# A hybrid pooling and Mamba-2 step on one core: the state-space chunk stage in one written order on all five engines, and the tail's gating moved into PSUM

## The chip, the cores and the metric

The kernel runs on one core of a Trainium2 chip. The metric is device time in microseconds (us) of one execution; a time is the median of several runs. Engines are named as in the profile: PE (TensorE), DVE (VectorE), ACT (ScalarE), POOL (GpSimd) and SP (SyncE, which here only issues loads).

## What is computed

One layer of a decoder for 1024 prompt rows and 64 sample rows, in float32. Cut to what the change concerns:

```
u_pool, z_pool, z_ssm, xbc, dt, g = split(h @ w_in)
P = (pool_mix(u_pool) * silu(z_pool)) @ w_pool_out
# state-space part: chunks of 128 rows, per group of 8 heads
att   = (C B^T) * exp(-(decay differences, lower triangle)) * dt
y     = att @ x  +  (C * exp(cumulated decay)) @ state
state = state * exp(last) + B^T @ (weight * dt * x)
v = (y + d_skip * x) * silu(z_ssm)
S = rmsnorm(v, ssm_norm_g) @ w_ssm_out
m = sigmoid(g_pool) * P + sigmoid(g_ssm) * S
out = x + gate * (m @ w_o);   then a final rmsnorm
```

## The kernel before

Data lies transposed: channels on the 128 partitions, 1088 rows (1024 + 64) along the free axis. Float32 products are made from three matmuls, high part by high, high by low and low by high (L360 to L362), so every operand is first split into a high and a low part: a copy on ACT, then a subtraction on POOL or DVE.

The program goes through adaLN and gates, the large projections, convolution and pooling, the **chunk stage** (about 826 to 1138 us of the profile), the **tail** (to 1201) and the output product.

*Chunk stage.* There are 4 groups of 8 heads and 8 chunks each, 32 chunks. One chunk's work, `chunk(g, c)`, is a generator of four steps: load xb (x, B and C) and the decay tile `dec`; exponentials (`cE` L1398, POOL's mask in `far` L1193, eight `exps` L1202 on ACT); turn (PE transposes x and B and makes B by C, L118 and L1409), weigh (`xd` L1418, `ps` L1419, `xw` L1421), mix (`dec` L1422 and `cE` L1424 are multiplied in place), low parts (`xwl` L1425, `btl` L1426), skip (`xD` L1429, ACT); then `inner` (PE, L1214 and L1217), the state update (PE L1435 to L1437, POOL L1442, DVE L1444), the sum (`v` L1448) and `finish` (DVE L1368, ACT L1369 and L1378, POOL L1370 to L1379), which leaves y split into Y. After a group's last chunk its state is transposed back and stored from an `xD` buffer (L1456, L1457).

Between these, PE makes **products**: blocks of 384, 352 and 352 columns, 12 matmuls each. The first 24 blocks are P (`P_unit`, evicted by DVE with a multiply, L1624), the following 72 belong to S of groups 0 to 2 (`S_unit`; group 0 copied by ACT, L1642; later ones added by DVE, L1645). A block rotates through three PSUM buffers, a chunk's own tiles through five others. `xd`, `xw`, `xwl`, `bt` and `btl` have one buffer each, `cE`, `xD` and the state two, `xb`, `dec` and `sz` three.

Only PE follows the written order here (`in_line`). Where DVE, ACT, POOL and SP put their instructions is decided by a scheduler, by what it expects to be ready, and by `behind`, which places a few of them after an engine's earlier work. Products are drawn by 2.56 blocks a chunk, four ahead of the first.

*Tail.* For each of eight 128-row slabs m, S of group 3 is multiplied (three blocks) and added to the sum `acc[m]` (a `G` tile; L1789), multiplied by gains that come from rstd in PSUM and the gate rows `R` (L1780, L1795), and P's part is added by POOL (L1796). The result is split for the output product (`m_split`, L1759 to L1771, its 64 sample columns in `sh`), and the output weights are loaded and split (`wo_split`, L1752 and L1753). The rstd of all rows is spread over the partitions by matmuls with nine diagonal tiles, which DVE makes (L1732). PE and DVE follow the written order in this stage.

Of the kernel before, what the change touches and what calls it, by code (L numbers as in the profile page):

```python
# [20 lines left out]
P = 128  # L21
# [25 lines left out]
def tile_pool_ssd_step(  # L47
# [1318 lines left out]
    def finish(g, o, S, v, sz):  # L1366

        V.tensor_tensor(v, v, sz, ALU.mult)  # L1368
        act(sz, v, AF.Square)  # L1369
        nc.gpsimd.tensor_tensor(sz[:, 0:2], sz[:, 0:2], sz[:, 2:4], ALU.add)  # L1370
# [6 lines left out]
        yhc = yh[g][:, :, o:o + S]  # L1377
        act(yhc, v, AF.Copy)  # L1378
        nc.gpsimd.tensor_tensor(yl[g][:, :, o:o + S], v, yhc.bitcast(F32), ALU.subtract)  # L1379

    def sample_end(g):
        sz = ckt([P, 4, P], "sz", 3)[:, :, :NS]
        load(sz, z_d[g][:, :, SEQ:])
        v = ckt([P, 4, P], "v")[:, :, :NS]
        load(v, ys_d[g])
        finish(g, SEQ, NS, v, sz)

    def chunk(g, c):
        o = c * P
        xb = ckt([P, 6, P], "xb", 3)  # L1390
        load(xb, xbc_d[g][:, :, o:o + P])
        Bf, Cf = xb[:, 4], xb[:, 5]
        dec = ckt([P, 8, P], "dec", 3)
        decays(dec, g, c)
        yield
        if c > 0:
            cE = ckt([P, 8, P], "cE")
            act(cE, dec, AF.Exp, scale=-1.0)  # L1398
        far(dec, c)
        exps(dec, g, c)  # L1400
        yield
        sz = ckt([P, 4, P], "sz", 3)
        load(sz, z_d[g][:, :, o:o + P])
        px = PB()
        for q in range(4):
            turn_r(px[:, q * P:(q + 1) * P], xb[:, q])
        pbc = PB()
        turn_r(pbc[:, :P], Bf)
        mm(pbc[:, P:2 * P], Bf, Cf, start=True, stop=True)  # L1409

        bth, btl = (ck.tile([P, P], F32R, tag=t, name=nm(t), bufs=1) for t in ("bt", "btl"))
        act(bth, pbc[:, :P], AF.Copy)
        if c > 0:
            act(pbc[:, 2 * P:3 * P], Cf, AF.Copy)
        pxv = px.rearrange("p (h d) -> p h d", d=64)
        heads = slice(8 * g, 8 * g + 8)
        xd = ckt([P, 8, 64], "xd", 1)
# [5 lines left out]
        if c > 0:  # L1423
            V.tensor_tensor(cE, cE, pbc[:, 2 * P:3 * P].unsqueeze(1).to_broadcast([P, 8, P]), ALU.mult)  # L1424
# [3 lines left out]
        for q in range(4):  # L1428
            act(xD[:, q], xb[:, q], AF.Copy, scale=Dv[:, 4 * g + q:4 * g + q + 1])  # L1429
# [512 lines left out]
```

## Time and profile before

| | |
|---|---|
| median of 3 runs | 1300.18 us (1298.1 to 1300.95) |
| the profiled execution | 1301.8 us |
| its span, first to last instruction | 1300.1 us |
| granted TensorE clock, mean | 0.994 |
| PE busy | 1258.6 us (97%) |
| DVE, ACT, POOL busy | 913.3, 709.5, 682.1 us |
| HBM traffic | 179 GB/s over the span |

Busy times are averages over stages with different limits, and matmuls overlap, so 97% does not say where PE stood still. Rows of a stretch of the span show that better: how much of 20 us PE was busy, at which clock, and how busy DVE, ACT and POOL were in the same 20 us. Where PE was held up, the chain of waits (from the last instruction back to what released each step) names the operation that came last.

### The profile page before, as it was taken

The page shows a single profiled execution, that of the slowest core. Times are in us where ns is not written, and L with a number is a line of the kernel's source. Part 1 is how long each engine was busy: PE and PEld are TensorE (multiplying, and loading weights), DVE is VectorE, ACT ScalarE, POOL GpSimd, SP SyncE. Part 2 cuts the span into 40 slices and gives each one's busy share as a digit, 9 for nine tenths or more (in the row PEclk, how much of TensorE's full clock was granted, in tenths as well). Part 3 has the DMA queues.
Part 4 walks back from the last instruction along what each step waited for, and adds up shares of the span by engine and source line. Part 5 has one row for each costly group of instructions (what it writes and reads, how often), then busy time and mean ns, then how long its engine had stood idle before and what let it go on. Part 6 is the DMA issues. An engine that isn't in the chain of part 4 may idle for free.

```text
span 1300.1 us, 26439 instructions
## 1 busy us (share of the span) xinstructions
PE 1258.6 (97%) x9771; PEld 1177.4 (91%) x9771; DVE 913.3 (70%) x1581; ACT 709.5 (55%) x1676; POOL 682.1 (52%) x555
## 2 busy tenths in 40 slices
PE   7999999999999999999999999999899999989998
PEld 6779999989999999998989899989899999989786
DVE  4685778866978678775757655587677889478533
ACT  4665356375656564546455454777797878122211
POOL 1007668677869776664344444255475657266000
PEclk9999999999999999999999999999999999999999
DMA  9736345465455544444645565998666665284421
GB/s 333 241 116 224 119 153 171 142 206 166 151 183 198 157 159 128 158 138 125 192 142 173 155 178 161 341 320 285 215 202 199 191 210 163 74 300 165 156 89 49
DMA packets 225731, 234.92 MB, mean 181 GB/s; under 512 B 30369, under 2 KB 177009, under 8 KB 225594
## 3 DMA queue, kind: packets, MB, share of 16 engines
q1 hardware_dynamic: 155808, 159.01, 38.8%
q10 hardware_dynamic: 69794, 74.22, 16.7%
q8 instruction: 77, 1.26, 0.4%
q14 instruction: 52, 0.43, 0.1%
HBM read 158.67 MB, written 74.62 MB: 179 GB/s over the span
## 4 chain that ended last, share of the span: by engine, by line
PE 75%; DVE 6%; DMA 6%; issue 5%; ACT 4%; POOL 3%; ACTq 0%; SPq 0%; POOLq 0%; DVEq 0%
PE ps L609 6%; PE ps L610 6%; PE ps L611 6%; PE mm L609 6%; PE mm L611 6%; PE mm L610 6%; PE mm L361 5%; PE mm L360 5%; PE mm L362 5%; PE ps L1214 2%; PE ps L1888 2%; PE ps L1890 2%; PE ps L1889 2%; POOL wlo L169 2%; PE ps L1217 2%
## 5 line engine op out<-in xcount | busy, mean ns | idle before, releaser
L169 POOL TENSOR_TENSOR wlo<-rawA,whi 128x512 fp32r<-128x512 f32 x120 | 185.6, 1552 | 185.1 <-ACT whi L166 101.2
L169 POOL TENSOR_TENSOR wlo<-raw,whi 128x512 fp32r<-128x512 f32 x92 | 151.0, 1649 | 126.9 <-ACT whi L166 97.3
L360 PE MATMUL mm<-Y,whi 128*128 128x352 f32 (+1 forms) x480 | 161.2, 336 | 2.9 <-DVE G L1789 2.7
L361 PE MATMUL mm<-Y,whi 128*128 128x352 f32 (+1 forms) x480 | 158.5, 330 | 2.7 <-POOL Y L1379 1.6
L362 PE MATMUL mm<-Y,wlo 128*128 128x352 f32 (+1 forms) x480 | 158.1, 329 | 0.0
L611 PE MATMUL mm<-Y,wlo 128*128 128x272 f32 x496 | 143.5, 290 | 3.7 <-POOL wlo L169 3.3
L609 PE MATMUL ps<-Y,whi 128*128 128x272 f32 x496 | 144.5, 291 | 2.1 <-ACT o L809 1.5
L609 PE MATMUL mm<-Y,whi 128*128 128x272 f32 x496 | 146.3, 295 | 0.2 <-ACT whi L166 0.2
L610 PE MATMUL ps<-Y,whi 128*128 128x272 f32 x496 | 143.1, 289 | 0.0
L610 PE MATMUL mm<-Y,whi 128*128 128x272 f32 x496 | 142.8, 288 | 0.0
L611 PE MATMUL ps<-Y,wlo 128*128 128x272 f32 x496 | 142.6, 288 | 0.0
L166 ACT ACTIVATE whi<-rawA 128x512 fp32r<-128x512 f32 x125 | 78.2, 626 | 97.4 <-PE ps L610 43.0
L1057 DVE SCALAR_TENSOR_TENSOR GA<-GA,cvT,GA 128x1112 f32<-128x1112 f32 x72 | 125.5, 1747 | 0.3
L166 ACT ACTIVATE whi<-raw 128x512 fp32r<-128x512 f32 x96 | 58.7, 626 | 92.7 <-DVE raw L555 42.8
L611 PEld LDWEIGHTS mm<-Y,wlo 128*128 128x128 f32 x496 | 93.4, 188 | 5.6 <-POOL wlo L169 4.6
L609 PEld LDWEIGHTS ps<-Y,whi 128*128 128x128 f32 x496 | 93.3, 188 | 3.8 <-ACT o L809 1.7
L360 PEld LDWEIGHTS mm<-Y,whi 128*128 128x128 f32 x480 | 91.3, 190 | 5.3 <-DVE G L1789 3.1
L361 PEld LDWEIGHTS mm<-Y,whi 128*128 128x128 f32 x480 | 91.3, 190 | 5.1 <-POOL Y L1379 1.9
L609 PEld LDWEIGHTS mm<-Y,whi 128*128 128x128 f32 x496 | 93.3, 188 | 2.1 <-issue 0.8
L610 PEld LDWEIGHTS mm<-Y,whi 128*128 128x128 f32 x496 | 93.4, 188 | 0.7 <-issue 0.6
L611 PEld LDWEIGHTS ps<-Y,wlo 128*128 128x128 f32 x496 | 93.5, 188 | 0.2 <-issue 0.2
L610 PEld LDWEIGHTS ps<-Y,whi 128*128 128x128 f32 x496 | 93.3, 188 | 0.3 <-issue 0.2
(454 smaller groups left out, 3852.4 us busy)
## 6 DMA issues: line engine op xcount, KB each, us to landing
rawA<-in_w_in SPq DMA_DIRECT2D x46, 512.0 KB
dec<-acs_d SPq DMA_DIRECT2D x32, 512.0 KB
xbc<-GA ACTq DMA_DIRECT2D x24, 512.0 KB
xb<-xbc SPq DMA_DIRECT2D x32, 384.0 KB
rawA<-in_w_in SPq DMA_DIRECT2D x32, 256.0 KB
pw<-in_w_ssm_out ACTq DMA_DIRECT2D x32, 256.0 KB
ws<-ph ACTq DMA_DIRECT2D x32, 256.0 KB
ws<-pw SPq DMA_DIRECT2D x32, 256.0 KB
```

The costliest lines, as they stand in the source:

```text
L166: ins = act(hi[:, :, :ncols], raw[:, :, :ncols], AF.Copy)
L169: (eng or nc.gpsimd).tensor_tensor(lo[:, :, :ncols], raw[:, :, :ncols], hi[:, :, :ncols].bitcast(F32), ALU.subtract)
L360: mm(ps[:, :n], a, rh[k][:, o:o + n], start=(k == 0), stop=False)
L361: mm(ps[:, :n], a, rl[k][:, o:o + n], start=False, stop=False)
L362: mm(ps[:, :n], b, rh[k][:, o:o + n], start=False, stop=(k == nk - 1))
L609: mm(p, hi, ah, start=(k == 0), stop=False)
L610: mm(p, hi, al, start=False, stop=False)
L611: mm(p, lo, ah, start=False, stop=(k == 3))
L1057: V.scalar_tensor_tensor(d[:, :n], rp[:, k:k + n], cvT[:, 24 * k + mc:24 * k + mc + 1], d[:, :n], ALU.mult, ALU.add)
L1214: mm(o[hh], xd[:S, 2 * q + hh, :], dec[:S, 2 * q + hh], start=True, stop=state is None)
L1217: mm(o[hh], state[:, h * 64:h * 64 + 64], cE[:, h], start=False, stop=True)
L1888: mm(ps[:, :cw], mhk, wo[k][0][:, s], start=(k == 0), stop=False)
```

## The change

The generator is taken apart into functions for single steps (`ch_turn`, `ch_weigh`, ...), and a loop over the 32 chunks writes out their order. In iteration i it issues turn, weigh, skip, mix and low parts of chunk i+1, the exponentials of chunk i+2, the loads of chunk i+3 (xb early, the decay tile after `inner(i)`), and `inner`, state update and finish of chunk i. `xd`, `xw`, `xwl`, `bt` and `btl` get a second buffer, `cE` a third. All five engines follow this order. Two product blocks stand ahead of the first chunk and three in each iteration, one before `inner(i)` and two at its end; in the last six iterations two. At a group's border the first two units' third blocks are moved behind their first two. Stores of finished P units are issued one iteration later, on ACT. Gate rows for the tail are loaded at i = 21, 26 and 28.

In the tail ACT makes the diagonal tiles, ACT and POOL follow the written order too, the gains of slab m+1 are made between the blocks of slab m, and from slab 1 on the gating reads PSUM: the sum of group 0 to 2 is added into the block's PSUM tile, and the product with the gain row goes from there to `acc`. POOL's sum stays; for the last slab DVE does all of it by blocks. The pool of `m` tiles has seven buffers instead of eight.

```diff
+    def ch_turn(i):
+        xb = xbs[i]
+        pxs[i], pbs[i] = PB(), PB()
+        for q in range(4):
+            turn_r(pxs[i][:, q * P:(q + 1) * P], xb[:, q])
+        turn_r(pbs[i][:, :P], xb[:, 4])
+        mm(pbs[i][:, P:2 * P], xb[:, 4], xb[:, 5], start=True, stop=True)
+        bts[i] = [ck.tile([P, P], F32R, tag=t, name=nm(t), bufs=2) for t in ("bt", "btl")]
+        act(bts[i][0], pbs[i][:, :P], AF.Copy)
+        if i % NC > 0:
+            act(pbs[i][:, 2 * P:3 * P], xb[:, 5], AF.Copy)
+    def ch_weigh(i):
+        g, c = divmod(i, NC)
+        heads = slice(8 * g, 8 * g + 8)
+        pxv = pxs[i].rearrange("p (h d) -> p h d", d=64)
+        xds[i] = ckt([P, 8, 64], "xd", 2)
+        V.tensor_tensor(xds[i], pxv, dtT[:, c, heads].unsqueeze(2).to_broadcast([P, 8, 64]), ALU.mult)
+        V.tensor_tensor(pxv, pxv, wdT[:, c, heads].unsqueeze(2).to_broadcast([P, 8, 64]), ALU.mult)
+        xws[i] = [ck.tile([P, 512], F32R, tag=t, name=nm(t), bufs=2) for t in ("xw", "xwl")]
+        act(xws[i][0], pxs[i], AF.Copy)
+    def ch_skip(i):
+        g = i // NC
+        xDs[i] = ckt([P, 4, P], "xD", 2)
+        for q in range(4):
+            act(xDs[i][:, q], xbs[i][:, q], AF.Copy, scale=Dv[:, 4 * g + q:4 * g + q + 1])
+        xbs.pop(i)
+    def ch_mix(i):
+        V.tensor_tensor(decs[i], decs[i], pbs[i][:, P:2 * P].unsqueeze(1).to_broadcast([P, 8, P]), ALU.mult)
+        if i % NC > 0:
+            V.tensor_tensor(cEs[i], cEs[i], pbs[i][:, 2 * P:3 * P].unsqueeze(1).to_broadcast([P, 8, P]), ALU.mult)
+    def ch_lows(i):
+        V.tensor_tensor(bts[i][1], pbs[i][:, :P], bts[i][0].bitcast(F32), ALU.subtract)
+        V.tensor_tensor(xws[i][1], pxs[i], xws[i][0].bitcast(F32), ALU.subtract)
+        pxs.pop(i), pbs.pop(i)
...
+    def ch_inner(i):
+        g, c = divmod(i, NC)
+        if c == 0:
+            yh[g], yl[g] = [Y4(hs if g % 2 else hp) for _ in range(2)]
+        pis[i] = inner(xds.pop(i), decs.pop(i), P, *((hst[g], cEs.pop(i)) if c > 0 else ()))
+        pus[i] = PB()
+        (bh, bl), (xh, xl) = bts.pop(i), xws.pop(i)
+        mm(pus[i], bh, xh, start=True, stop=False)
+        mm(pus[i], bl, xh, start=False, stop=False)
+        mm(pus[i], bh, xl, start=False, stop=True)
+    def ch_out(i):
+        vs[i] = ckt([P, 4, P], "v", 2)
+        V.tensor_tensor(vs[i], pis.pop(i), xDs.pop(i), ALU.add)
+        ch_state(i)
+        V.tensor_tensor(vs[i], vs[i], szs[i], ALU.mult)
+    def ch_state(i):
+        g, c = divmod(i, NC)
+        hn = hnew.pop(i)
+        if c == 0:
+            V.tensor_copy(hn, pus.pop(i))
+        else:
+            V.tensor_tensor(hn, hn, pus.pop(i), ALU.add)
+        hst[g] = hn
...
+    def state_out(g):
+        pt = PB()
         for q in range(4):
...
+            nc.tensor.transpose(pt[:, q * P:(q + 1) * P], hst[g][:, q * P:(q + 1) * P], ident)
+        fo = ckt([P, 4, P], "xD", 2)
+        act(fo, pt.rearrange("p (q n) -> p q n", n=P), AF.Copy)
+        store_(new_ssm_p[0, 0, 8 * g:8 * g + 8].rearrange("(q h) p n -> (h p) q n", h=2), fo)
...
+    turns = [(u, j) for u in range(8) for j in range(3)]
+    for g in range(1, NG):
+        turns += [(8 * g + u, j) for u, j in ((0, 0), (0, 1), (1, 0), (1, 1), (0, 2), (1, 2))]
+        turns += [(8 * g + u, j) for u in range(2, 8) for j in range(3)]
...
-    RATE = 2.56
-    FRONT = 4
...
+    FRONT = 2
+    def products(n):
...
-        while made < RATE * t:
+        while made < n:
...
-    in_line((mybir.EngineType.PE,), True)
-    with behind(mybir.EngineType.Activation):
-        next(seq[1])
-    for _ in range(FRONT):
-        next(pc_)
-    next(seq[0])
-    for i in range(len(seq)):
-        if i + 1 < len(seq):
-            with behind(mybir.EngineType.DVE, 1 - i) if i < 2 else ExitStack():
-                next(seq[i + 1])
-        products(i + 0.4)
-        if i > 0:
-            next(seq[i - 1], None)
-        next(seq[i], None)
-        if i % NC == 3:
-            sample_end(i // NC)
-        if i + 3 < len(seq):
-            next(seq[i + 3])
-        if i + 2 < len(seq):
-            with behind(mybir.EngineType.Activation) if i == 0 else ExitStack():
-                next(seq[i + 2])
-        products(i + 1.0)
-    next(seq[-1], None)
+    ENGS = (mybir.EngineType.PE, mybir.EngineType.DVE, mybir.EngineType.Activation, mybir.EngineType.Pool, mybir.EngineType.SP,)
+    in_line(ENGS, True)
+    z_load(0)
+    ch_turn(0)
+    ch_weigh(0)
+    ch_far(1)
+    ch_skip(0)
+    ch_mix(0)
+    ch_lows(0)
+    ch_exps(1)
+    products(FRONT)
+    ch_decay(0)
+    for i in range(NCH):
+        g, c = divmod(i, NC)
+        if i + 1 < NCH:
+            ch_turn(i + 1)
+            ch_weigh(i + 1)
+        if c == 0 and i > 0:
+            state_out(g - 1)
+        if i + 1 < NCH:
+            z_load(i + 1)
+        if i + 3 < NCH:
+            ch_load(i + 3)
+        if not False and i + 2 < NCH:
+            ch_far(i + 2)
+        if i + 1 < NCH:
+            ch_skip(i + 1)
+        flush()
+        products(FRONT + 3 * i + 1 - max(0, i - 25))
+        if not False and i + 2 < NCH:
+            ch_exps(i + 2)
+        if i + 1 < NCH:
+            ch_mix(i + 1)
+            ch_lows(i + 1)
+        ch_inner(i)
+        if i + 3 < NCH:
+            d_load(i + 3)
+        if False and i + 2 < NCH:
+            ch_far(i + 2)
+        ch_out(i)
+        y_act(g, c * P, vs[i], szs[i])
+        if False and i + 2 < NCH:
+            ch_exps(i + 2)
+        if i + 1 < NCH:
+            ch_decay(i + 1)
+        y_pool(g, c * P, vs.pop(i), szs.pop(i))
+        early(i)
+        if c == 2:
+            sample_load(g)
+        if c == 3:
+            sample_end(g)
+        products(FRONT + 3 * i + 3 - max(0, i - 25))
+    next(pc_)
+    state_out(NG - 1)
     for _ in pc_:
         pass
-    in_line((mybir.EngineType.PE,))
+    flush()
+    in_line(ENGS)
     right.__exit__(None, None, None)
...
-        V.tensor_scalar(dg, ident[:n, :n], rs9[:n, c:c + 1], None, ALU.mult)
+        act(dg, ident[:n, :n], AF.Copy, scale=rs9[:n, c:c + 1])
...
+    def gains(m):
+        for j, ps in enumerate(rstd):
+            s = slice(512 * j, min(512 * j + 512, T))
+            V.tensor_tensor(rows_r[m][:, s], ps[:, :s.stop - s.start], rows_r[m][:, s], ALU.mult)
     def m_done(m):
-        r = R()
-        load(r, gs_d[m])
-        def gains():
-            for j, ps in enumerate(rstd):
-                s = slice(512 * j, min(512 * j + 512, T))
-                V.tensor_tensor(r[:, s], ps[:, :s.stop - s.start], r[:, s], ALU.mult)
-        if m == 7:
-            gains()
         mt = M()
         load(mt, m1_d[m])
-        a = acc[m]
+        a, r = acc[m], rows_r[m]
         def done(o, n, ps):
             s = slice(o, o + n)
-            V.tensor_tensor(a[:, s], ps[:, :n], a[:, s], ALU.add)
+            if m == 0:
+                V.tensor_tensor(a[:, s], ps[:, :n], a[:, s], ALU.add)
+                if o + n == T:
+                    gains(0)
+                    V.tensor_tensor(a, a, r, ALU.mult)
+                    nc.gpsimd.tensor_tensor(a, a, mt, ALU.add)
+                return
+            V.tensor_tensor(ps[:, :n], ps[:, :n], a[:, s], ALU.add)
             if m < 7:
-                s = slice(0, T)
-                if o + n < T:
-                    return
-                gains()
-            V.tensor_tensor(a[:, s], a[:, s], r[:, s], ALU.mult)
-            (nc.gpsimd if m < 7 else V).tensor_tensor(a[:, s], a[:, s], mt[:, s], ALU.add)
+                V.tensor_tensor(a[:, s], ps[:, :n], r[:, s], ALU.mult)
+                if o + n == T:
+                    nc.gpsimd.tensor_tensor(a, a, mt, ALU.add)
+            else:
+                V.tensor_tensor(ps[:, :n], ps[:, :n], r[:, s], ALU.mult)
+                V.tensor_tensor(a[:, s], ps[:, :n], mt[:, s], ALU.add)
...
     def tail_unit(m):
         pf, run_ = S_unit(3, m, m_done)
         def run(w):
-            for _ in run_(w):
-                pass
-            wo_load(m)
-            if m < 6:
-                wo_split(m, M)
+            k = m + EARLY
+            if k < 8:
+                wo_load(k, M((P, D)))
+            if 0 < m < 6:
+                r_load(m + 2)
+            run_(w, 0)
+            if m == 0:
+                run_(w, 1)
+                run_(w, 2)
+            if m < 7:
+                gains(m + 1)
             if m > 0:
+                run_(w, 1)
                 m_split(m - 1, M8 if m < 5 else G)
+            if m < 4:
+                wo_split(k, w4[0][:, m, :D], w4[1][:, m, :D])
+            elif k < 8 and m < 6:
+                wo_split(k, M((P, D), F32R), M((P, D), F32R))
+            if m > 0:
+                run_(w, 2)
             if m > 1:
                 samples[m - 2]()
...
-    in_line((mybir.EngineType.PE, mybir.EngineType.DVE), True)
+    in_line((mybir.EngineType.PE, mybir.EngineType.DVE, mybir.EngineType.Activation, mybir.EngineType.Pool,), True)
```

How this moves instructions, at three places.

DVE, one chunk in the middle of the stage, before the change (L1418 and L1419 weigh, L1422 and L1424 mix, L1425 and L1426 low parts, L1448, L1444 and L1368 the sum, state and gate of the chunk that PE has just made, L1645 product blocks):

```order
L1418 TENSOR_TENSOR xd_14336<-ps_14324,dtT 128x512
L1419 TENSOR_TENSOR ps_14324<-ps_14324,wdT 128x512
L1448 TENSOR_TENSOR v_14407<-ps_14383,xD_14234 128x512
L1444 TENSOR_TENSOR hst_14404<-hst_14404,ps_14400 128x512
L1368 TENSOR_TENSOR v_14407<-v_14407,sz_14210 128x512
L1425 TENSOR_TENSOR xwl_14340<-ps_14324,xw_14339 128x512
L1422 TENSOR_TENSOR dec_14167<-dec_14167,ps_14329 128x1024
L1424 TENSOR_TENSOR cE_14295<-cE_14295,ps_14329 128x1024
L1426 TENSOR_TENSOR btl_14333<-ps_14329,bt_14332 128x128
L1645 TENSOR_TENSOR G_13280<-mm_14433,G_13280 128x352
L1645 TENSOR_TENSOR G_13280<-mm_14476,G_13280 128x352
```

After it (L1426 and L1427 weigh, L1439 and L1441 mix, L1444 and L1445 low parts, L1468, L1478 and L1470 sum, state and gate, L1698 product blocks):

```order
L1426 TENSOR_TENSOR xd_14476<-ps_14464,dtT 128x512
L1427 TENSOR_TENSOR ps_14464<-ps_14464,wdT 128x512
L1698 TENSOR_TENSOR G_12356<-mm_14500,G_12356 128x352
L1439 TENSOR_TENSOR dec_14296<-dec_14296,ps_14465 128x1024
L1441 TENSOR_TENSOR cE_14367<-cE_14367,ps_14465 128x1024
L1444 TENSOR_TENSOR btl_14473<-ps_14465,bt_14472 128x128
L1445 TENSOR_TENSOR xwl_14480<-ps_14464,xw_14479 128x512
L1468 TENSOR_TENSOR v_14549<-ps_14526,xD_14372 128x512
L1478 TENSOR_TENSOR hst_14430<-hst_14430,ps_14543 128x512
L1470 TENSOR_TENSOR v_14549<-v_14549,sz_14363 128x512
L1698 TENSOR_TENSOR G_12537<-mm_14561,G_12537 128x384
L1698 TENSOR_TENSOR G_12537<-mm_14575,G_12537 128x352
```

Mix and low parts of the next chunk stood behind the sum and gate of the chunk before, and now stand ahead of them, with one product block in front of them and two at the end.

ACT at the first group border, before (L1412, L1414 and L1421 the copies of turn and weigh, L1456 and L1457 the state's copy and store, L1642 copies of product blocks, L1369 and L1378 finish, L1429 skip, L1398 cE):

```order
L1412 ACTIVATE bt_12307<-ps_12304 128x128
L1414 ACTIVATE ps_12304<-xb_12137 128x128
L1421 ACTIVATE xw_12314<-ps_12299 128x512
L1456 ACTIVATE xD_12345<-ps_12340 128x512
L1642 ACTIVATE G_12282<-mm_12391 128x352
L1457 DMA out<-xD_12345 128x4x128
L1642 ACTIVATE G_12409<-mm_12410 128x384
L1369 ACTIVATE sz_12173<-v_12365 128x512
L1378 ACTIVATE Y_12348<-v_12365 128x4x128
L1642 ACTIVATE G_12409<-mm_12453 128x352
L1429 ACTIVATE xD_12448<-xb_12246,Dv 128x128 x4
L1398 ACTIVATE cE_12504<-dec_12376 128x1024
```

After (L1417, L1419 and L1429 copies of turn and weigh, L1501 and L1502 the state, L1402 cE, L1435 skip, L1679 a store of P, L1695 product blocks, L1202 exps, L1482 and L1483 finish):

```order
L1417 ACTIVATE bt_12319<-ps_12312 128x128
L1419 ACTIVATE ps_12312<-xb_12085 128x128
L1429 ACTIVATE xw_12326<-ps_12311 128x512
L1501 ACTIVATE xD_12334<-ps_12329 128x512
L1502 DMA out<-xD_12334 128x4x128
L1402 ACTIVATE cE_12341<-dec_12270 128x1024
L1435 ACTIVATE xD_12346<-xb_12085,Dv 128x128 x4
L1679 DMA m_164<-R_12049 128x1088
L1695 ACTIVATE G_12356<-mm_12357 128x384
L1202 ACTIVATE dec_12270<-dec_12270,acT 128x128 x8
L1482 ACTIVATE sz_12209<-v_12400 128x512
L1483 ACTIVATE Y_12383<-v_12400 128x4x128
```

Between the store and the next skip there stood product copies and finish; now there stands only cE, and the first product copy stands behind the skip.

DVE in the tail, one slab, before (L1789 sums into `acc`, L1780 gains, L1795 multiply, L1760 and L1771 low parts of the slab before):

```order
L1789 TENSOR_TENSOR G_12564<-mm_15438,G_12564 128x384
L1789 TENSOR_TENSOR G_12564<-mm_15452,G_12564 128x352
L1789 TENSOR_TENSOR G_12564<-mm_15466,G_12564 128x352
L1780 TENSOR_TENSOR R_15434<-ps_15275,R_15434 128x512
L1780 TENSOR_TENSOR R_15434<-ps_15276,R_15434 128x512
L1780 TENSOR_TENSOR R_15434<-ps_15277,R_15434 128x64
L1795 TENSOR_TENSOR G_12564<-G_12564,R_15434 128x1088
L1760 TENSOR_TENSOR sh_15489<-G_12409,sh_15489 128x64
L1771 TENSOR_TENSOR m_2617_15493<-G_12409,m_2616_15492 128x1024
```

After (L1888 sums in PSUM, L1890 multiply out of PSUM, L1872 gains of the next slab, L1855 and L1866 low parts of the slab before):

```order
L1888 TENSOR_TENSOR mm_15449<-mm_15449,G_12537 128x384
L1890 TENSOR_TENSOR G_12537<-mm_15449,R_14903 128x384
L1872 TENSOR_TENSOR R_15377<-ps_15281,R_15377 128x512
L1872 TENSOR_TENSOR R_15377<-ps_15282,R_15377 128x512
L1872 TENSOR_TENSOR R_15377<-ps_15283,R_15377 128x64
L1888 TENSOR_TENSOR mm_15467<-mm_15467,G_12537 128x352
L1890 TENSOR_TENSOR G_12537<-mm_15467,R_14903 128x352
L1855 TENSOR_TENSOR sh_15482<-G_12356,sh_15482 128x64
L1866 TENSOR_TENSOR m_2618_15486<-G_12356,m_2617_15485 128x1024
L1888 TENSOR_TENSOR mm_15491<-mm_15491,G_12537 128x352
L1890 TENSOR_TENSOR G_12537<-mm_15491,R_14903 128x352
```

The multiply over all 1088 columns from SBUF is replaced by three from PSUM, and the low parts stand ahead of the third block.

More of the change, by code (lines that the diff above doesn't have):

```diff
@@ L1370, in finish, with y_pool @@
+    def y_pool(g, o, v, sz):
+        S = v.shape[2]
         nc.gpsimd.tensor_tensor(sz[:, 0:2], sz[:, 0:2], sz[:, 2:4], ALU.add)
@@ L1590, in to_chunks @@
         right_all.append(right)
-        seq.extend(chunk(g, c) for g in range(NG) for c in range(NC))
-        next(seq[0])
+        seq.append(0)
+        ch_load(0)
+        d_load(0)
     first_ws, first_g = {}, []
```

219 lines of the change are left out of this document (98 added, 121 removed).

## The prediction

> **What bounds the kernel now.** First the stretches of the span, 20 us each. Columns: length, busy us (instructions) of PE, weight load, DVE, ACT and POOL, granted TensorE clock, share of the DMA engines, GB/s.
>
> ```profile
> 840.00:860.00 20.00, 17.48 (x149) 15.89 (x149) 16.07 (x26) 14.29 (x41) 9.40 (x10) 1.00 0.98 329
> 880.00:900.00 20.00, 19.85 (x166) 18.50 (x165) 17.48 (x27) 16.31 (x49) 11.58 (x12) 1.00 0.94 318
> 900.00:920.00 20.00, 18.06 (x129) 16.35 (x128) 13.70 (x24) 13.32 (x35) 8.46 (x9) 0.91 0.68 211
> 920.00:940.00 20.00, 18.43 (x158) 16.99 (x156) 12.13 (x18) 14.17 (x39) 10.28 (x12) 1.00 0.64 206
> 1040.00:1060.00 20.00, 20.00 (x159) 18.87 (x159) 17.26 (x28) 13.89 (x37) 10.93 (x12) 1.00 0.71 219
> 1160.00:1180.00 20.00, 15.58 (x81) 14.91 (x82) 18.00 (x21) 3.49 (x6) 14.63 (x6) 0.91 0.51 168
> ```
>
> TensorE bounds it. The change touches only the chunk stage (about 826 to 1138) and the tail behind it (to 1201), and within them PE loses time in two places: 840 to 940, and 1155 to 1168. Around 1050 it is full. PE's instructions are the same after the change, so only waits and half-clock stretches can go or come.
>
> How much the first place costs is seen by comparing equal work. The chain of waits shows the first state-update matmul of a chunk (L1435); the groups in each stretch count the product matmuls.
>
> ```profile
> 848.74 0.43 PE ps L1435
> 934.83 0.43 PE ps L1435
> 951.88 0.43 PE ps L1435
> 985.37 0.43 PE ps L1435
> 994.77 0.43 PE ps L1435
> 1028.90 0.43 PE ps L1435
> ```
>
> ```profile
> L360 PE MATMUL mm<-Y,whi 128*128 128x352 f32 (+1 forms) x92 | 31.7, 344 | 0.2 <-ACT Y L1378 0.2
> ...
> L360 PE MATMUL mm<-Y,whi 128*128 128x352 f32 (+1 forms) x92 | 30.8, 335 | 0.0
> ```
>
> Nine chunks and 23 product blocks (92 / 4) lie between 848.74 and 934.83, 86.09 us, and the same between 951.88 and 1028.90, 77.02 us, with one group border in each. So the early stretch loses **9.1 us**. One clean chunk with three blocks is 994.77 - 985.37 = 9.40 us.
>
> The chain names the losers (start, length, what):
>
> ```profile
> 856.71 1.21 DVE dec L1422
> 857.92 1.14 DVE cE L1424
> ...
> 900.29 6.98 DMA xb<-xbc
> 907.28 1.93 ACT dec L1202 x7
> ...
> 914.06 1.24 POOL Y L1379
> ...
> 918.38 8.67 DMA out<-xD
> 927.38 0.97 ACT xD L1429 x3
> 928.36 0.95 ACT cE L1398
> ...
> 930.67 1.13 DVE dec L1422
> ```
>
> Each time, work on a chunk's decay tile (L1202, L1422, L1424) ends just when PE wants it, because it is made just before use: a late load of xb, or a store that holds an xD buffer, reaches PE undamped. At 914 PE waits for POOL's last write of Y, with which the first product of a group begins; the clock falls to 0.91 in that window, 0.09 x 20 = 1.8 us, which is part of the 9.1.
>
> **The tail.** From the chain a unit's three gains, and two starts of the sample matmuls, one unit apart where PE is not held up; then groups of tile G between 1140 and 1205 (ns: min/median/max); then PE's waits there.
>
> ```profile
> 1154.64 1.34 DVE R L1780 x3
> ...
> 1173.20 0.93 PE ps L1765 x4
> 1180.05 0.93 PE ps L1765 x4
> ```
>
> ```profile
> L1789 DVE TENSOR_TENSOR G<-mm,G x24: 506/525/553, 1142.1 to 1203.1; 128x352 f32<-128x352 f32 x16, 128x384 f32<-128x384 f32 x8
> L1795 DVE TENSOR_TENSOR G<-G,R x10: 526/1365/3457, 1150.1 to 1203.6; 128x1088 f32<-128x1088 f32 x7, 128x352 f32<-128x352 f32 x2, 128x384 f32<-128x384 f32 x1
> L1796 POOL TENSOR_TENSOR G<-G,m x7: 2489/3585/3602, 1153.2 to 1197.0; 128x1088 f32<-128x1088 f32 x7
> L1759 ACT ACTIVATE sh<-G x7: 257/257/259, 1155.8 to 1200.7; 128x64 fp32r<-128x64 f32 x7
> L1770 ACT ACTIVATE m<-G x4: 1039/1043/1045, 1156.0 to 1182.5; 128x1024 fp32r<-128x1024 f32 x4
> L1771 DVE TENSOR_TENSOR m<-G,m x4: 1210/1215/3529, 1161.5 to 1184.0; 128x1024 fp32r<-128x1024 f32 x4
> ```
>
> ```profile
> PE mm L360 <- DVE G L1789: 2.7, 1, 2.7
> PE ps L1765 <- DVE sh L1760: 1.8, 1, 1.8
> ```
>
> PE waits 2.7 + 1.8 us, and window 1160 to 1180 has the clock at 0.91, another 1.8: **6.3 us**. DVE is late there because its operations on two SBUF operands (L1795, L1771) take up to 3.46 and 3.53 us instead of their medians of 1.365 and 1.215, while the sums that read PSUM (L1789) never leave 0.51 to 0.55. POOL runs beside the long ones.
>
> The Trainium skill, page "SBUF — State Buffer", section "SBUF: two separate sides", has DVE with two SBUF inputs and GpSimd exclude each other from one port pair, each for its whole instruction. The trace agrees: 3.5 against 1.2 us, and only on such operations. By that rule the split (two SBUF inputs before and after) could be blocked in every unit, and the tail would give back up to 2.3 us a unit; by the row it is not, since its median is 1215 ns and only the longest is 3529.
>
> **The change, part by part.**
>
> *A whole chunk of lead.* Weighting, mix and low parts of chunk i+1 now stand in front of inner(i), in second buffers, so their result is used 9 us later rather than at once. The three stalls at 856, 907 and 930 have causes shorter than that: 1.9 us (L1202), 2.4 us (1.21 + 1.14), and ACT's wait for the store, below. I let the 9.1 us go, and charge what is new:
>
> - Start. The first chunk is now turned, weighted and mixed ahead of two products, and PE meets turn(2) after about a chunk, while ACT still has two exp batches and a table load to do.
>
> ```profile
> L1202 ACT ACT_TABLE_LOAD x1 | 1.3, 1283 | 0.4 <-ACT u L721 0.4
> ```
>
>   From nothing to one table load and one batch (1.28 + 1.93 = 3.2 us); I take **1.2**.
> - Group border. After the state store ACT's next xD needs a buffer that the store still reads; the scheduler could put other work first, the written order can't. ACT stands for up to 8.67 - 0.95 (the cE exp between them) = 7.7 us, at the first border with product copies (L1695) queued behind it. Less half a chunk of lead (4.7), PE waits 0 to 3.0, with the half clock's 1.8 up to 4.8; the later borders copy on DVE. I take **1.0**.
> - Transfers beside the gate products, at 0.94 to 0.98 of the DMA engines in the first windows. Three blocks a chunk instead of 2.56 raise only the products' part of the bytes. The decay tile is now loaded most of a chunk before use (before: a whole one), and xb above took 6.98. So 0 (all in time) to 3 us (0.4 in each of eight chunks); I take **0.4**.
> - The last six chunks have two blocks and so less PE time to hide DVE. The busy sums of the whole chunk stage, and from 940 to 1110 the copies of a product block:
>
> ```profile
> 825.00:1138.00 313.00, 304.71 (x2457) 283.14 (x2457) 233.67 (x363) 225.45 (x612) 166.47 (x194) 0.99 0.67 214
> ```
>
> ```profile
> L1645 DVE TENSOR_TENSOR G<-mm,G 128x352 f32<-128x352 f32 x22 | 10.8, 513 | 1.1 <-PE mm L362 1.1
> L1642 ACT ACTIVATE G<-mm 128x352 f32<-128x352 f32 x12 | 5.3, 452 | 0.2 <-PE mm L362 0.2
> ```
>
>   DVE takes 72 of the 96 blocks (0.52 each, 37), so a chunk is (233.67 - 37) / 32 = 6.1 us: with three blocks 7.7 of PE's 9.4, with two 7.2 of 7.5. ACT: (225.45 - 24 x 0.46) / 32 = 6.7, with three copies 8.1. POOL 5.2. Everyone fits, with 0.3 us to spare at the end: 0 to 3 us, I take **0**.
>
> Chunk stage: -9.1 + 1.2 + 1.0 + 0.4 = **-6.5 us**.
>
> *Two or three blocks a chunk in one pattern*, z and state work on other places of the queues: the same instructions; nothing, covered by the slack above.
>
> *Tail.* Gating in PSUM takes the multiply of L1795 (1.365 to 3.457) off the blocked kind and adds three PSUM-source multiplies (0.525 each, as L1789). DVE per unit: six of these 3.2, gains 1.3, split 1.4 (1.2 and its small piece for the samples), sum 5.9, against PE's 6.85 (1180.05 - 1173.20, of which 0.93 for the samples and 5.92 for three blocks). POOL's sum is then free to run its 2.49. The 6.3 us go. But unit 0 keeps the old way, and DVE's written order puts the split of unit 0 ahead of unit 1's last block: 0.5 (sum) + 1.3 (gains) + 1.4 (multiply) + 2.5 (POOL) + 1.3 (ACT, 0.26 + 1.04) + 1.4 (split) + 1.1 (block) = 9.5 us after unit 0, while PE reaches the third block of unit 2, whose PSUM buffer that block frees, after 5.9 + 3.9 = 9.8: 0 to 2.3 (one blocked operation), I take 1.3. In each later unit the same circle (block, POOL 2.5, ACT 1.3, split, block) is within half a microsecond of PE's 6.85; I take 0.4 in four units, 1.6 (0 to 3). The diagonal on ACT instead of DVE is nine small operations either way. Tail: -6.3 + 2.9 = **-3.4 us**, bounds -6.3 and, with the split blocked as now, 0.
>
> A rule of the Trainium skill speaks against it: by "Perfetto Trace Analysis", section "Optimizing Scalar/DVE Operations", DVE pays about 125 ns per PSUM access against 60 on SBUF; three short multiplies instead of one long would by that page cost an estimated 0.3 us more per unit. The rows agree (3 x 0.525 against 1.365).
>
> **Sum.** -6.5 - 3.4 = -9.9 us. The profiled execution took 1301.8 us (span 1300.1), which gives 1291.9. The median of the runs, 1300.18, lies 1.6 under it, so **1290.3 us**.
>
> **The rivals.**
>
> *Larger gain.* All new charges are nothing: -15.4, some 1285. For it: every charge starts at 0. Against: five engines with 0.3 to 1.7 us of spare time per chunk. Chance 0.10.
>
> *No difference.* The change does not do what it says: the border stalls return as ACT standing behind the state store (4.8), the start takes 3.2, the transfers 3, and the tail gains nothing because POOL, now in written order too, is again beside DVE's split. -15.4 + 4.8 + 3.2 + 3 + 6.3 = +1.9, some 1302; with half of these terms larger gains remain, so within 0.2% (2.6 us, about what a measurement of this kernel can tell) I give 0.13.
>
> *Slower: DVE in written order becomes the bound.* The scheduler let DVE do whatever was ready; now an eviction behind a waiting mix waits too, and PE's three PSUM buffers fill.
>
> ```profile
> DVE xd L1418 <- PE ps L1214: 38.4, 29, 4.8
> DVE G L1645 <- PE mm L362: 20.3, 17, 1.8
> ```
>
> DVE already waits 38.4 + 20.3 = 58.7 us in the stage, 1.8 per chunk, for PE, and PE does not wait for it. 7.7 + 1.8 = 9.5 against 9.4 is 0.1 us too long if these waits all stay; if written order lengthens them by half, to 2.7, it is 1.0. The middle, 0.5 us in 26 chunks, is 13 us: 1301.8 - 9.9 + 13 = 1304.9, in runs about 1303. It decides from 9.9 / 26 = 0.38 us per chunk. Against it: the waits of 38.4 are those of an engine with nothing to do, and shrink when it has. Chance 0.19.
>
> **How the numbers follow.** Forecast 0.58, larger gain 0.10, no difference 0.13, slower 0.19. Faster 0.68, same 0.13, slower 0.19. The bounds of the charges alone give 1285 (all nothing) to 1302 (all full); the range goes on to the slower case's middle: 1284 to 1303, which leaves out half of that case and little below.
>
> **What will show it.** In the changed profile: PE windows of 840 to 940 at 19.5 or more with the clock at 1.00; state-update matmuls 9.4 us apart from the start; no chain step on the mix lines (L1439, L1441); the chunk stage some 6 us shorter. ACT's wait for the state store in the list of waits, and whether PE's products wait for ACT behind it. In the tail, the PSUM multiplies (L1890) at 0.5 us throughout, and PE's waits for them below 3 us in sum. Wrong it would be by a wait of PE for DVE or ACT in every chunk, or if the stage is DMA-bound up to 900, so that PE waits for weights or decay loads that the old order hid.

## The result, and the profile after

| | before | after |
|---|---|---|
| median | 1299.94 us (1298.1 to 1300.95, 4 runs) | 1290.19 us (1289.25 to 1292.2, 4 runs) |
| ratio | | 0.9929, 95% interval 0.9911 to 0.9946 |
| the profiled execution's span | 1300.1 us | 1290.4 us |
| granted clock, mean | 0.994 | 0.995 |

The change saves 9.8 us; 1290.3 was forecast. Whether it saves them where the forecast put them is another question, and the first thing to look at is where the stages end. The last projection matmul (L611) and the matmuls that sum the squares at the tail's start (L1723, after the change L1834) mark the chunk stage. A row of this view ends with the first and last start of the group; before, then after:

```profile
L611 PE MATMUL ps<-Y,wlo x496: 282/288/393, 83.2 to 825.3; 128*128 128x272 f32 x166
...
L1723 PE MATMUL ps<-ones,sq_acc x18: 165/250/250, 1137.7 to 1139.5; 128*128 128x1 f32 x16, 128*64 128x1 f32 x2
```

```profile
L611 PE MATMUL ps<-Y,wlo x496: 282/288/393, 83.7 to 826.6; 128*128 128x272 f32 x166
...
L1834 PE MATMUL ps<-ones,sq_acc x18: 165/250/250, 1130.7 to 1132.6; 128*128 128x1 f32 x16, 128*64 128x1 f32 x2
```

| stretch | before | after | difference |
|---|---|---|---|
| span's start to the last projection | 825.3 | 826.6 | +1.3 |
| chunk stage | 312.4 | 304.1 | -8.3 |
| tail and output, to the span's end | 162.4 | 159.7 | -2.7 |

The first line is no effect of the change: PE's instructions there are the same, and in the experiments below, which leave them as they are too, this stretch lasted between 820.2 and 825.8 us. So a span carries up to some 6 us of scatter (820.2 to 826.6) from a place that nobody touched, and stages are the better measure. They scatter too, but less: the same chunk-stage program took 302.7 us in e1 and 304.0 in e6, against 304.1 here.

The windows of the changed kernel (columns as in the prediction):

```profile
820.00:840.00 20.00, 19.09 (x141) 17.94 (x140) 10.43 (x17) 15.32 (x32) 4.48 (x3) 1.00 0.83 289
840.00:860.00 20.00, 17.87 (x142) 16.51 (x141) 17.11 (x26) 18.06 (x50) 10.91 (x11) 0.91 0.92 289
...
880.00:900.00 20.00, 20.00 (x165) 18.91 (x165) 16.37 (x27) 13.48 (x38) 9.98 (x11) 1.00 0.97 325
...
1140.00:1160.00 20.00, 17.50 (x103) 16.70 (x102) 18.11 (x31) 4.31 (x6) 11.04 (x5) 1.00 0.82 290
```

```profile
860.00:1120.00 260.00, 260.00 (x2158) 244.62 (x2156) 205.38 (x319) 198.80 (x533) 153.73 (x178) 1.00 0.70 220
```

From 860 to 1120 PE is busy 260.00 of 260 us at full clock: the stalls at 907 and 930 are gone, and nothing has come in their place, at the group borders or in the last chunks. What is left stands mainly at two places, 840 to 860 with a lowered clock, and 1140 to 1160. The waits name them (the first three from the chunk stage, the last from the tail):

```profile
ACT xD L1435 <- DMA out<-xD: 2.5, 3, 0.9
...
PE ps L118 <- DVE btl L1444: 2.1, 1, 2.1
...
PE ps L1214 <- DVE dec L1439: 0.6, 1, 0.6
```

```profile
PE mm L360 <- DVE G L1890: 2.5, 1, 2.5
```

The 2.1 us are PE at the turn of chunk 2, which needs the PSUM tile that DVE's low part of chunk 1 still reads; with the clock at 0.91 in that window (0.09 x 20 = 1.8 us) the stall costs 3.9 in this execution. The 1.8 do not come every time. e1, e6 and e12, described below, have the same program here and the same wait of 2.1 us, some two to four microseconds earlier: from 840 to 850 the granted clock is 0.83 in this profile and in e6, but 1.00 in e1 and e12. The 2.5 us are a product block of slab 2 that waits for the gating of slab 1.

### The profile page after: what moved, and what is told of

It is laid out like the page before. It is cut to its first block, busy times and chain, and to the rows that moved or that the text cites. A ratio compares the mean times of both kernels' runs of the same rounds, so it can differ in the third digit from the quotient of the medians.

```text
span 1290.4 us, 26363 instructions
## 1 busy us (share of the span) xinstructions
PE 1255.1 (97%) x9771; PEld 1176.8 (91%) x9771; DVE 911.8 (71%) x1584; ACT 718.4 (56%) x1685; POOL 675.5 (52%) x555
## 5 line engine op out<-in xcount | busy, mean ns | idle before, releaser
L611 PE MATMUL mm<-Y,wlo 128*128 128x272 f32 x496 | 143.7, 290 | 4.1 <-POOL wlo L169 3.6
L611 PE MATMUL ps<-Y,wlo 128*128 128x272 f32 x496 | 142.6, 288 | 0.0
L611 PEld LDWEIGHTS mm<-Y,wlo 128*128 128x128 f32 x496 | 93.4, 188 | 6.0 <-POOL wlo L169 4.9
L611 PEld LDWEIGHTS ps<-Y,wlo 128*128 128x128 f32 x496 | 93.5, 188 | 0.2 <-issue 0.2
```

Of the source, the lines that this page charges most:

```text
L611: mm(p, lo, ah, start=False, stop=(k == 3))
```

## The experiments

Ratios are to the kernel before, each run beside it on one chip, with the 95% interval. The chunk stage is measured by the same two groups as above, from starts with two decimals, so a tenth can differ from what the printed rows give. It comes from one profiled execution of each run, the median from all of them.

| run | median, us | ratio | chunk stage, us |
|---|---|---|---|
| e1: new chunk stage, old tail | 1290.28 | 0.9932 (0.9917 to 0.9946) | 302.7 |
| e2: old chunk stage, new tail | 1298.30 | 0.9989 (0.9977 to 1.0002) | 314.3 |
| e3: single buffers | 1296.14 | 0.9971 (0.9957 to 0.9985) | 311.0 |
| e4: only PE in written order | 1327.58 | 1.0217 (1.0200 to 1.0235) | 341.3 |
| e5: four blocks ahead | 1289.24 | 0.9925 (0.9907 to 0.9944) | 302.6 |
| e6: early weight splits | 1286.59 | 0.9895 (0.9879 to 0.9912) | 304.0 |
| e7: e5 and e6 | 1286.99 | 0.9905 (0.9891 to 0.9920) | 304.6 |
| e8: xd weighed three times | 1293.62 | 0.9951 (0.9933 to 0.9969) | 307.9 |
| e9: e6, four blocks ahead of the mix | 1284.57 | 0.9884 (0.9857 to 0.9912) | 301.1 |
| e10: PE and ACT in written order | 1295.45 | 0.9961 (0.9946 to 0.9976) | 310.3 |
| e11: all but ACT in written order | 1304.86 | 1.0041 (1.0023 to 1.0059) | 318.2 |
| e12: group borders in plain order | 1289.63 | 0.9920 (0.9892 to 0.9947) | 303.4 |

### The two halves apart

e1 has the new chunk stage and all of the old tail:

```diff
-    mq = open_("mq", 7)
+    mq = open_("mq", 8)
...
-        act(dg, ident[:n, :n], AF.Copy, scale=rs9[:n, c:c + 1])
+        V.tensor_scalar(dg, ident[:n, :n], rs9[:n, c:c + 1], None, ALU.mult)
...
-            V.tensor_tensor(ps[:, :n], ps[:, :n], a[:, s], ALU.add)
+            V.tensor_tensor(a[:, s], ps[:, :n], a[:, s], ALU.add)
```

> The new chunk stage with the tail as it was before (gating through SBUF, diagonal on DVE, eight m buffers). Theory: the two halves of the change are independent, and the chunk stage gave about 8 us of the gain (projections' end to the first row-sum matmul: 312.3 us before, 304.1 after). So about 1292 us, and in the tail the two PE waits of before (1.8 and 2.7 us) return. Rival: the tail's gain is what shows and the chunk stage's is given back behind it (gate rows loaded late, POOL still busy): then 1296 to 1298.

e2 is the old chunk stage with the new tail; its three first gate rows are loaded ahead of the tail.

> The old chunk stage with the new tail. Theory of independent halves: about 2.5 us under the kernel before, 1297.5 us. Rival: the tail alone gives nothing (1300), because its remaining stall of 2.7 us at the split of slab 0 is the old one moved.

e1 took 1290.28 us: the chunk stage alone gives practically the whole gain. e2 took 1298.30, -1.2 us with an interval from -3.0 to +0.3. So the independence that was expected holds as far as these runs can tell, but the tail's share is smaller than forecast and can't be told from nothing by their medians. In e1's tail the wait of 2.7 us is back as expected, the one of 1.8 with only 0.5. In e2's tail there is one wait, the same as after the change, where before there were two of 2.7 and 1.8:

```profile
PE mm L360 <- DVE G L1808: 2.5, 1, 2.5
```

### The second buffers

```diff
-        xds[i] = ckt([P, 8, 64], "xd", 2)
+        xds[i] = ckt([P, 8, 64], "xd", 1)
...
-            cEs[i] = ckt([P, 8, P], "cE", 3)
+            cEs[i] = ckt([P, 8, P], "cE", 2)
```

and `bufs=1` for xw, xwl, bt and btl.

> The change, with xd, xw, xwl, bt and btl back to one buffer and cE to two, everything in the same written order. Theory of the lead: the buffers make the order possible; without them DVE's weighing of chunk i+1 waits for inner(i) and ACT's xw for the state update, DVE's work of 7.7 us then starts half a chunk later, and PE waits in some chunks: 1293 to 1300. Rival of throughput: what counts is that 7.7 us of DVE fit into 9.4 of PE, wherever they begin: 1290, no chunk longer than 9.4.

It took 1296.14 us, two thirds of the gain lost, but not by a loss in each chunk. Windows of e3 (from an execution of 1298.82 us, the longest of its ten, so its losses are at the upper end):

```profile
860.00:900.00 40.00, 40.00 (x332) 37.80 (x331) 33.88 (x55) 29.50 (x82) 21.16 (x25) 1.00 0.91 300
900.00:940.00 40.00, 36.91 (x281) 34.36 (x280) 22.03 (x34) 26.71 (x70) 17.91 (x21) 0.91 0.70 227
940.00:1060.00 120.00, 120.00 (x994) 112.89 (x993) 91.31 (x142) 90.46 (x250) 71.17 (x85) 1.00 0.62 194
1080.00:1120.00 40.00, 38.84 (x337) 35.43 (x336) 37.22 (x58) 34.15 (x94) 28.61 (x35) 1.00 0.68 208
```

```profile
PE mm L360 <- ACT G L1695: 3.1, 1, 3.1
```

Between 940 and 1060 PE is as full as with two buffers: in the steady part the rival was right, what fits fits. The loss is at the first group border, where PE's product block waits 3.1 us for ACT's copy of an earlier one (L1695) and the clock falls to 0.91 (0.09 x 40 = 3.6 us), and 1.2 us in the last six chunks, where DVE is busy 37.22 of 40. ACT is late at the border for two reasons: its first copy of the turned chunk (L1417) waits 1.9 us until PE is done with the single buffer, and its skip (L1435) then waits 2.7 us for the state store. In e1, with two buffers, ACT waits 3.6 us for the same store, and PE is still busy 260.00 of the 260 us from 860 to 1120. The lead is thus insurance: it pays where something is late, not in a chunk by itself.

### Whose order

```diff
-    ENGS = (mybir.EngineType.PE, mybir.EngineType.DVE, mybir.EngineType.Activation, mybir.EngineType.Pool, mybir.EngineType.SP,)
+    ENGS = (mybir.EngineType.PE,)
```

> The change, but in the chunk stage only PE follows the written order; DVE, ACT, POOL and SP are placed by the scheduler again. Theory of the lead: PE's order and the second buffers carry the gain, the rest of the order little: 1290 to 1293. Rival: the written order of the other engines is the gain, since the scheduler puts mix behind other work as before: 1297 to 1300, with stalls between 840 and 940 as before.

It took 1327.58 us, 28 more than before the change: the theory of the lead fell, and the rival was right beyond its numbers. The scheduler's own order, without the `behind` placements that the old program had, nearly all of them at its first chunks, loses 37 us in the chunk stage. Much of that is lost at the start, where PE stands 13.5 of 40 us and the clock takes another 0.17 x 40 = 6.8 (after the change 3.0 and 1.8):

```profile
820.00:860.00 40.00, 26.52 (x189) 24.52 (x188) 20.91 (x33) 27.54 (x67) 9.55 (x8) 0.83 0.74 255
```

No run put those placements back into the new program, so how much of the 37 us they alone would save stays open. Waits of e4 (the first from ACT, the other two from PE):

```profile
ACT cE L1402 <- DMA dec<-acs_d: 40.6, 19, 5.5
```

```profile
PE ps L1214 <- DVE dec L1439: 15.0, 2, 13.1
PE ps L118 <- DVE btl L1444: 9.1, 4, 3.9
```

ACT waits for the decay tile 19 times, and what stands behind it on its queue is late with it. Two further runs take ACT and the others apart:

```diff
+    ENGS = (mybir.EngineType.PE, mybir.EngineType.Activation,)
```

> The change with only PE and ACT in written order in the chunk stage; DVE, POOL and SP placed by the scheduler. With PE alone it took 1327.6 us, and ACT there stood 40.6 us for decay loads with the copies of a turned chunk queued behind. Theory that ACT's order is what counts: 1290 to 1295. Rival, DVE's and SP's order: 1315 or more.

```diff
+    ENGS = (mybir.EngineType.PE, mybir.EngineType.DVE, mybir.EngineType.Pool, mybir.EngineType.SP,)
```

> The change with PE, DVE, POOL and SP in written order in the chunk stage and only ACT placed by the scheduler. Theory that ACT's order is what counts: 1315 or more, with PE's long wait at the first mix. Rival, the other engines' order: 1290 to 1300.

e10 took 1295.45 us, e11 1304.86. ACT's order alone takes 31 of the 37 us away (341.3 to 310.3), the order of DVE, POOL and SP alone 23 (to 318.2): ACT's counts for more, as the theory said, but it is not the whole: e10 lies just over its 1290 to 1295, and e11's 1304.86 well under the 1315 that was expected. The shares overlap, since 31 and 23 are more than 37; that a late ACT hurts most where DVE also stands in a bad order would fit, but is not shown. What is left in e10, and then in e11:

```profile
PE ps L1214 <- DVE dec L1439: 4.2, 1, 4.2
...
PE mm L360 <- ACT G L1695: 2.3, 1, 2.3
```

```profile
PE ps L1214 <- DVE dec L1439: 8.5, 1, 8.5
PE ps L1217 <- DVE hst L1478: 4.1, 4, 2.1
```

In both the start's first mix is late. In e10 ACT also stands behind the state store at the borders, up to 4.6 us at a time, and its product copies with it:

```profile
ACT xD L1435 <- DMA out<-xD: 8.0, 3, 4.6
```

### Is DVE in written order near its limit?

```diff
         V.tensor_tensor(xds[i], pxv, dtT[:, c, heads].unsqueeze(2).to_broadcast([P, 8, 64]), ALU.mult)
+        V.tensor_tensor(xds[i], pxv, dtT[:, c, heads].unsqueeze(2).to_broadcast([P, 8, 64]), ALU.mult)
+        V.tensor_tensor(xds[i], pxv, dtT[:, c, heads].unsqueeze(2).to_broadcast([P, 8, 64]), ALU.mult)
```

> The change with DVE's weighing of xd (0.69 us, from PSUM) issued three times in each chunk, to the same tile: 1.4 us more of DVE per chunk, the output unchanged. Theory of throughput: DVE's 7.7 + 1.4 = 9.1 us still fit under PE's 9.4 in the first 26 chunks and cost nothing; in the last six 7.2 + 1.4 - 7.5 = 1.1 us each, together 7: 1297 us. Rival (written order adds DVE's waits of 1.8 us per chunk to its work): 9.1 + 1.8 - 9.4 = 1.5 us in each of 26 chunks and more at the end: over 1325.

It took 1293.62 us. Windows of e8:

```profile
860.00:1060.00 200.00, 200.00 (x1640) 188.20 (x1635) 181.14 (x278) 150.71 (x407) 114.28 (x131) 1.00 0.73 224
...
1080.00:1120.00 40.00, 36.04 (x308) 32.78 (x305) 37.92 (x58) 25.66 (x69) 26.18 (x34) 1.00 0.52 160
```

With DVE busy 181 of 200 us PE does not lose a hundredth; only in the last chunks, with two blocks each, is DVE too slow, and PE stands 4.0 us. This is throughput, and it ends the slower rival of the prediction: DVE's waits do not add to its work, they shrink as the work grows (from 860 to 1060 DVE was idle 48.3 us after the change, 18.9 here). The loss at the end was expected at 7 us; the chunk stage grew by 3.8. Work done ahead may carry the first of these chunks, but that is not shown.

### Group borders

```diff
-        turns += [(8 * g + u, j) for u, j in ((0, 0), (0, 1), (1, 0), (1, 1), (0, 2), (1, 2))]
-        turns += [(8 * g + u, j) for u in range(2, 8) for j in range(3)]
+        turns += [(8 * g + u, j) for u in range(8) for j in range(3)]
```

> The change with the products of a group in plain order, the third block of its first two units not moved. The third block reads the last chunks' Y. Theory: moved by two blocks (4 us) it waits for nothing; in plain order PE waits 1 to 3 us for POOL's last Y at each of three borders: 1293 to 1297. Rival: the whole chunk of lead covers this too: 1290.

It took 1289.63 us, and PE is busy 259.80 of the 260 us between 860 and 1120. The rearranged blocks are worth nothing that can be measured here: POOL's last Y is done in time without them.

### The two stalls that are left

```diff
-    FRONT = 2
+    FRONT = 4
```

> The change with four product blocks ahead of the first chunk instead of two. Theory: the one stall left in the changed chunk stage (turn of chunk 2 at 841.6 us waits 2.1 us for DVE's low part, which waits for ACT's late exponentials, and a half-clock stretch follows, 3.9 us in all) is ACT's start being late by a fixed time; two blocks, 4 us, cover it: 1286.5 us, the chunk stage 300.3. Rival: the stall moves with PE's order, or the early blocks wait for their weights and gate rows: 1290.

It took 1289.24 us, no difference from the change that can be told. The wait at the turn of chunk 2 is gone, and another has come:

```profile
PE mm L360 <- DVE R L1670: 1.9, 1, 1.9
```

L1670 is DVE's eviction of a P block. With four blocks written behind `ch_mix(0)`, the evictions stand behind a mix that starts at 831.31, just after ACT's late copy of B (L1417, 830.95 to 831.23), and PE runs out of its three PSUM buffers. So the rival was right in that the stall moved.

The other stall, in the tail, e6:

```diff
+            if m == 0:
+                for e in range(2):
+                    wo_split(e, w4[0][:, e, :D], w4[1][:, e, :D])
                 run_(w, 1)
                 run_(w, 2)
...
-            if m < 4:
+            if 1 < m < 4:
                 wo_split(k, w4[0][:, m, :D], w4[1][:, m, :D])
```

with both raw loads in the first slab.

> The change with the output weights' splits 0 and 1 both made in the tail's first slab, ahead of its second block, when POOL is idle; the second slab makes none. Theory of the port: the tail's one stall (PE 2.5 us behind the gating of slab 1) is the split L1866, 3.42 instead of 1.23 us, because POOL's weight split runs beside it; with POOL quiet there the split takes 1.23, the stall goes, 1287.5 us. Rival: the circle of block, POOL, ACT and split is too long at slab 1 by itself; L1866 stays long or PE waits over 1.5 us all the same: 1290.

It took 1286.59 us, and in its tail PE waits for no engine. DVE's split L1866 in the changed kernel, and in e6:

```profile
L1866 DVE TENSOR_TENSOR m<-G,m x4: 1224/1226/3417, 1149.4 to 1172.3; 128x1024 fp32r<-128x1024 f32 x4
```

```profile
L1866 DVE TENSOR_TENSOR m<-G,m x4: 1218/1226/1226, 1147.6 to 1168.2; 128x1024 fp32r<-128x1024 f32 x4
```

The one split that took 3.4 us has become as short as the others by taking POOL's work out of its time. In the changed kernel POOL's two weight splits (L1730) ran from 1147.02 to 1151.78; DVE's split began at 1149.45, beside the second of them, and ended at 1152.87, 1.1 us behind it, about its own length when alone. In e6 POOL does nothing while the same split runs, and in e7 and e9, which have this edit too, the longest of these splits takes 1.23 us. The Trainium skill (page "SBUF — State Buffer", section "SBUF: two separate sides") has the two engines lock each other out for a whole instruction in such a case. The trace agrees with it.

e7 has both edits.

> Both of the above: four blocks ahead, and the weight splits 0 and 1 early. If the two stalls are independent, 3.9 + 2.7 = 6.6 us under the changed kernel, 1283.6; if the start's stall only moves, 1287.5; if neither theory holds, 1290.

It took 1286.99 us: the tail's gain and not the start's, the second of the three cases (1287.5). The last run takes e6 and mends the start's order:

```diff
-    FRONT = 2
+    FRONT = 4
...
+    products(2)
     ch_turn(0)
     ch_weigh(0)
     ch_far(1)
     ch_skip(0)
+    products(FRONT)
     ch_mix(0)
     ch_lows(0)
     ch_exps(1)
-    products(FRONT)
```

> The early weight splits of the run before, and four blocks at the start, but two of them ahead of the first chunk's turn and two ahead of its mix, so that DVE evicts them before it waits in the mix. Theory: with four blocks behind the mix PE waited 1.9 to 2.4 us for their evictions (L1670), which stood behind DVE's mix; in this order neither that wait nor the one at the turn of chunk 2 is left, the chunk stage takes 300.3 us and the whole 1283. Rival: DVE and ACT are late for the first chunks in any order, and PE waits 2 us or more elsewhere before 850: 1287.

It took 1284.57 us, the lowest median of all, 1.2% under the kernel before. The intervals of e9, e7 and e6 overlap, so that the start is mended is read from the profile: the chunk stage is 2.9 us shorter than in e6 and 3.5 shorter than in e7. Of PE's waits for engines one is left from the end of the projections to the output, at the stage's first block, and the windows are full:

```profile
PE mm L361 <- DVE Y L1516: 1.0, 1, 1.0
```

```profile
840.00:860.00 20.00, 20.00 (x169) 18.83 (x168) 17.43 (x30) 16.22 (x43) 12.33 (x13) 1.00 1.02 348
860.00:1120.00 260.00, 259.82 (x2151) 243.67 (x2151) 203.65 (x313) 197.08 (x526) 154.11 (x180) 1.00 0.69 210
1140.00:1160.00 20.00, 19.92 (x117) 18.95 (x116) 17.87 (x36) 5.52 (x8) 11.03 (x6) 1.00 0.67 224
```

The chunk stage, 301.1 us, is 0.8 us above the forecast. With the share of the DMA engines at 1.02 in 840 to 860 PE still misses nothing.

## Why the prediction was right, and where it was not

- **The old stalls go.** Forecast -9.1 us; right, and too small. Against e9's stage (301.1), in which PE is full from 840 to 1120, the old one lost some 11 us: the comparison of two stretches had left out the losses outside the first. The stage fell by 8.3 and not by 11, because of the new stall at its start.
- **Why they go.** The prediction put it on the lead and the second buffers, and the forecast did not rest on whose order it is. By e3 the buffers for the lead are worth 6.9 us at most (311.0 against 304.1), at one border and at the end, while by e4 the order of the engines beside PE, of which ACT's is the larger part, decides between 304 and 341 us. Whose order it is was the step with the thinnest reason, and much hangs on it; what share of it the old `behind` placements would have kept is open.
- **Start, +1.2, bounds 0 to 3.2.** Mis-sized: PE waits 2.1 us in all four profiles of this program start (the change, e1, e6, e12), and with the lower clock behind it 3.9 in the one shown; e9, without this stall, has a stage 1.6 us (e1) to 3.0 us (this profile) shorter. The mechanism was named rightly, ACT's late exponentials at the turn of chunk 2: behind its first batch ACT loads a table twice (1.28 us each, at 831.40 and 834.69), because the last activation of the projections (L721) stands between the batches. The prediction had one load. The half clock behind the stall was left out of the sum, and whether it comes differs between these four.
- **Group border, +1.0.** 0, with the right mechanism. In this profile ACT waits 0.9 us at most for the store, where before it waited up to 5.7:

```profile
ACT xD L1429 <- DMA out<-xD: 10.6, 3, 5.7
```

  The 8.7 us that were taken as the store's time are not its time under the new order: from its issue to the skip that needs the buffer there are 2.4 us here and 5.1 in e1. A lead of half a chunk (4.7 us), as the prediction had it, fits e1, where 3.6 us of waiting cost PE nothing. In e10, with DVE, POOL and SP left to the scheduler, 4.6 us of waiting cost PE 2.3, and in e3, with less lead, 2.7 cost it 3.1.
- **Transfers, +0.4.** 0: PE is full at a share of 0.97, and in e9 at 1.02.
- **End, 0.** Right: PE is full to 1120.
- **Tail, -3.4.** -2.7 in the profile, -1.2 (-3.0 to +0.3) alone in e2. By the profiles the gain is real: from the first square-sum matmul to the span's end the nine runs that have this tail unchanged took 159.7 to 161.8 us, the two with the old one 162.4 and 163.8. The size lies nearer to 2 than to 3.4. One stall was expected from the first slab's split, 1.3 us of 0 to 2.3, and measured at 2.5; the upper bound with one blocked operation was the case. The later slabs, 1.6, wait for nothing: this wait is the only one in the tail.
- **The sum.** -8.3 and -2.7 are 1.1 us more than forecast; the 1.3 us of the stretch ahead, which is scatter, hide that in this profile. That the median met the forecast within 0.1 us is partly luck: the old stalls were taken too small, the start too small as well, and border, transfers and later slabs too large.
- **The slower rival** (DVE in written order) falls by e8; **no difference** by the result; the **larger gain** was to be had, by e6 and e9, with two small moves.

## What to carry to other kernels

Where one engine is the bound and the rest fit under it, write down the order of all of them, the copies' engine first, and let each wait fall a whole step ahead of its use; in this kernel the extra buffers then protected a border and the end and were worth nothing in between. At a stage's start look for what stands behind a waiting instruction: here two blocks written ahead of it, so that their evictions did not stand behind it, helped, and the same two written behind it did not. And when DVE's operations on two SBUF tensors vary threefold in length, see what POOL does beside them, and move that.

## What was not expected of the hardware

- The share of the DMA engines reached 1.02 in 840 to 860 of e9 (348 GB/s) with PE full: a busy share near one is not a sign that anybody waits.
- The stretch ahead of the chunk stage, the same instructions for PE in every program, ended between 820.2 and 826.6 us. The cause stays open.
- A short wait of PE can cost nearly its length again, but need not. The same wait of 2.1 us at the turn of chunk 2 was followed by a lower clock in two profiles (this one and e6, 0.83 from 840 to 850; here 0.50 from 846 to 848) and by none in two others (e1 and e12, 1.00). The 3.1 us in e3 were followed by one (0.91 in the 40 us around), the 2.5 us at 1151 were not (1.00 in its window). The Trainium skill, page "TensorE: Matmul & The Clock Gate", section "What's actually happening", says that the gate watches windows of activity of about 3.4 us that run freely. By the table in that section of the Trainium skill the clock falls after at least one idle window. That the same wait goes both ways agrees with windows that run freely; that 2.1 us, less than a window, can be enough is more than the table says, and here the measurement decides.
